# A seven-product matrix multiply and its seam: weight differences and splits from GpSimd to VectorE, and a product reordered by token tile

## The chip, the cores and the metric

The kernel runs on one core of a Trainium2 chip. A core has a matrix engine (TensorE, PE in the profile, with its weight loads as PEld), a vector engine (VectorE, DVE), a scalar engine (ScalarE, ACT), a general engine (GpSimd, POOL) and a queue that issues transfers between the chip's main memory and the on-chip memory (SyncE, SP). Each engine works through its own instructions in a fixed order and waits on semaphores for the others. Matrix results land in PSUM, in banks of 128 x 512 float32; all else lives in SBUF. The metric is the time on the device in microseconds (us), the median over runs.

## The reference

One layer of a bidirectional encoder over 1024 tokens of width 1024, in float32. Each of its three sub-layers is wrapped in RMS norms, and the normed result is added to the residual:

```
x = x + rms(mix(rms(x)) @ w_out)                  # window attention and gated DeltaNet, in parallel
c = softmax(q k^T / 16) v @ w_co                  # 4-head cross-attention to 256 memory tokens
x = x + rms(c) * g_cross_post
f = (silu(h @ w_gate) * (h @ w_up)) @ w_down      # h = rms(x) * g_ffn_pre
x = x + rms(f) * g_ffn_post
```

The change touches the product with `w_co` (1024 x 1024), the norm and residual behind it, and what prepares its result for the feed-forward part.

## The kernel before

**Splits.** Every float32 matrix product is made of three products of rounded parts. `split(hi, lo, src)` (lines 100 to 107) lets ScalarE cast the source to the rounded part `hi` (L103) and another engine subtract it from the source to get `lo` (L104): VectorE, unless the caller names GpSimd with `eng=`. `three` (L1254) then adds hi x hi, hi x lo and lo x hi into one bank. So each operand costs one ScalarE and one VectorE or GpSimd instruction before TensorE can use it.

**The w_co product.** Tokens, inner dimension and output columns are each halved, and the four blocks of the activations (q0, q1, of the two token halves) and of the weights (b11, b12, b21, b22) are combined by a scheme that needs seven block products instead of eight, with sums and differences of blocks around them. A block product is 512 tokens (four token tiles of 128) x 512 inner rows (four of 128, `HK`) x 512 columns: 48 matmuls into four banks. In order they are: a11 with B11 and a12 with B21 (both with weights loaded as they are), s3 with b12, a22 with b21, the s2 part with b22, s1 with b11, and s4 with B22 loaded again. Between the first ones, `sums` and `later` form the weight differences in place, four steps of two each; each is one `minus` of 128 x 512 (L1275), sixteen in all, on GpSimd. `weight_part` (line 1237) splits one 128 x 512 row block of a formed weight; its parts come from a ring of nine slots, tag `wpart`, and it is marked as more urgent than its place in the program. `act_part` splits the activation blocks in the same way, two row blocks at a time.

**The order of the loops.** `block_product` goes over the four inner row blocks outside and the four token tiles inside, so all four banks are complete only in the last quarter. The last product (s4) is written out by hand with the token tiles outside: each bank is complete before the next one begins.

**Finishing a token tile.** When the last term of a tile is in, VectorE adds it up (L1318), ScalarE squares it for the norm (`square_of`, L1279), the post gain is multiplied in (L1321), and `finish` loads the residual (L1288, SP), forms the reciprocal root of the mean square on GpSimd in two tiny steps (L1290 and L1291), adds the scaled tile to the residual on VectorE (L1292), stores it (L1293, SP), squares the sum on ScalarE (L1295), forms the second reciprocal root on GpSimd (L161 and L162) and scales, on ScalarE for even tiles (L1299) and VectorE for odd ones (L1301). The second half of the tokens (tiles 4 to 7, in `zl`) is finished behind the s1 product, the first half (`zz`) behind s4.

**The seam.** The code behind it turns these tiles with TensorE transposes (L1376), eight groups of the tokens in `zl` first, each group needing all four tiles. For `zl`, ScalarE multiplies in the gain (L1387) and each group is split into x1h and x1l, the `lo` part on GpSimd for even groups and VectorE for odd ones. For `zz`, four steps form X22 and the sums T1 to T4 that the seven-product scheme of the feed-forward part needs; the `lo` parts of T2 and T4 are made on GpSimd. Beside this, the first four column blocks of the feed-forward product that need only x1h and x1l (`EARLY`, banks `pA`, L1421) already run.

**What sets the order.** The instructions of one engine run in the order a planner writes at compile time, from a model of their times and the urgency of each; it is not changed at run time. Weight loads (`load_w`, L126) and weight and activation parts are marked as urgent by 300 places.

Of the kernel before, what the change touches and what calls it, by code (L numbers as in the profile page):

```python
# [14 lines left out]
ALU = mybir.AluOpType  # L15
# [4 lines left out]
P = 128  # L20
# [56 lines left out]
def tile_hybrid_block(  # L77
# [22 lines left out]
    def split(hi, lo, src, scale=None, eng=None):  # L100

        if scale is None:
            nc.scalar.copy(hi, src)  # L103
            (eng or nc.vector).tensor_tensor(lo, src, f32(hi), ALU.subtract)  # L104
        else:
            nc.scalar.activation(hi, src, AF.Identity, scale=scale)
            nc.vector.scalar_tensor_tensor(lo, src, scale, f32(hi), ALU.mult, ALU.subtract)
# [1129 lines left out]
    def weight_part(b_, k):  # L1237
        with tc.high_priority(AHEAD):
            dh, dl = (rg.tile([P, HALF], F32R, tag="wpart", name="wpart", bufs=9) for _ in range(2))
            split(dh, dl, b_[:, k])  # L1240
        return dh, dl
# [14 lines left out]
    def block_product(banks, a, b_, first=True, last=True, extra=None):  # L1256

        for k in range(HK):
            if k % 2 == 0:
                ah, al = act_part(a, k)  # L1260
            if isinstance(b_, tuple):
                if k % 2 == 0:
                    rows, c0 = (HK * b_[0] + k) * P, HALF * b_[1]
                    wh, wl = load_w(w_co[rows:rows + 2 * P, c0:c0 + HALF], 2, HALF)
                dh, dl = wh[:, k % 2], wl[:, k % 2]
            else:
                dh, dl = weight_part(b_, k)
            for t in range(4):
                three(banks[t], ah[:, k % 2], al[:, k % 2], dh, dl, slice(t * P, (t + 1) * P), first and k == 0,
                      last and k == HK - 1, first and last)  # L1270
            if extra:
                extra(k)

    def minus(o_, a, b_):
        nc.gpsimd.tensor_tensor(o_, a, b_, ALU.subtract)  # L1275

    def square_of(src, ch, r):
        jk = tz.tile([P, HALF], F32, tag="junk", name="junk")
# [2 lines left out]
    def finish(r, z, eng):  # L1281

        tok = slice(r * P, (r + 1) * P)
        if 4 <= r < 6:
            xr = xr45[:, r - 4]
        else:
            xr = tz.tile([P, D], F32, tag="xr", name="xr", bufs=2)
        nc.sync.dma_start(xr, d_x1[tok, :])  # L1288
        rs = tz.tile([P, 1], F32, tag="prs", name="prs", bufs=4)
        nc.gpsimd.tensor_scalar(rs, ssq[:, 1, r:r + 1], ssq[:, 0, r:r + 1], D * EPS, ALU.add, ALU.add)  # L1290
        nc.gpsimd.tensor_tensor(rs, rs, mhalf[:, 0:1], ALU.pow)  # L1291
        nc.vector.scalar_tensor_tensor(xr, z, rs, xr, ALU.mult, ALU.add)  # L1292
        nc.sync.dma_start(d_x2[tok, :], xr)  # L1293
        s2 = tz.tile([P, 1], F32, tag="ps2", name="ps2", bufs=4)
        nc.scalar.activation(z, xr, AF.Square, accum_out=s2)  # L1295
        r2 = tz.tile([P, 1], F32, tag="pr2", name="pr2", bufs=4)
        rstd_of(r2, s2, 1.0 / D, EPS)
        if eng is nc.scalar:
            nc.scalar.activation(z, xr, AF.Identity, scale=r2)  # L1299
        else:  # L1300
            nc.vector.tensor_scalar(z, xr, r2, None, ALU.mult)  # L1301
# [15 lines left out]
    def add(o_, a, b_):  # L1317
        nc.vector.tensor_tensor(o_, a, b_, ALU.add)  # L1318
# [31 lines left out]
        add(e_[:, t], e_[:, t], X[t])  # L1350
    xr45 = opB3.tile([P, 2, D], F32, tag="b30", name="xr45")
    Z = four([PG] * 4)
    block_product(Z, s1_, b11, last=False)
    for t in range(4):
        add(za[:, t], za[:, t], Z[t])
        square_of(za[:, t], 1, 4 + t)
        gained(za[:, t], za[:, t], HI, nc.vector)
        finish(4 + t, zl[:, t], (nc.scalar, nc.vector)[t % 2])
# [26 lines left out]
    for k in range(KT):  # L1385
        pt = turned_k(first_rows, k)
        nc.scalar.activation(raw[:, k, :], pt, AF.Identity, scale=gain("ffn", k))  # L1387
        split(x1h[:, k, :], x1l[:, k, :], raw[:, k, :], eng=(nc.gpsimd, nc.vector)[k % 2])
    tr = LR2.enter_context(pool("tr", 1, side="right"))
    T2, T4 = (blocks(t) for t in operand(opA, "s0"))  # L1390
    T1, T3 = (blocks(t) for t in operand(opB, "s2"))
# [2 lines left out]
    for k in range(HK):  # L1394
        p0, p1 = turned_k(last_rows, k), turned_k(last_rows, k + HK)
        g0, g1 = gain("ffn", k), gain("ffn", k + HK)
        x12, t1, t2_, t3_ = (tr.tile([P, HALF], F32, name=f"r{i}", tag=f"r{i}") for i in range(4))
        t4 = raw[:, k + HK]
        nc.scalar.activation(x12, p0, AF.Identity, scale=g0)
        nc.vector.scalar_tensor_tensor(t1, p0, g0, raw[:, k], ALU.mult, ALU.subtract)  # L1400
        nc.vector.scalar_tensor_tensor(t3_, p1, g1, x12, ALU.mult, ALU.subtract)
        nc.vector.scalar_tensor_tensor(t2_, p1, g1, t1, ALU.mult, ALU.subtract)
        split(X22[0][:, k], X22[1][:, k], p1, g1)
        split(T1[0][:, k], T1[1][:, k], t1)
        split(T3[0][:, k], T3[1][:, k], t3_)
        nc.vector.tensor_tensor(t4, t4, t2_, ALU.subtract)
        split(T2[0][:, k], T2[1][:, k], t2_, eng=nc.gpsimd)
        split(T4[0][:, k], T4[1][:, k], t4, eng=nc.gpsimd)


    NF = FF // P
# [343 lines left out]
```

## Time and profile before

| | |
|---|---|
| median of three runs | 1540.01 us (1538.43 to 1542.44) |
| profiled execution | 1542.75 us, span 1541.0 us |
| mean granted TensorE clock | 0.987 |
| busy: TensorE, VectorE, ScalarE, GpSimd | 1479.5, 1106.6, 746.9, 436.5 us |
| w_co product (L1254) in the span | 766 to 873.5 us |
| seam and early feed-forward blocks | 873.5 to about 944 us |

A row of a group of instructions names line, engine, operation and tiles (out<-in), then shape and count, busy time and mean ns of one, and the idle time of that engine just before them with what ended it. A row of the timeline begins with the start and the length in us. A row of the waits says who waited for whom: total us, times, longest. A row of busy time by stretch gives the stretch, its length, the busy time and the number of instructions of each engine, the granted clock (1.00 is full), the DMA share and GB/s. A row of one tile gives shortest, median and longest ns, and the first and last start.

### The profile page before, as it was taken

The page shows a single profiled execution, that of the slowest core. Times are in us where ns is not written, and L with a number is a line of the kernel's source. Part 1 is how long each engine was busy: PE and PEld are TensorE (multiplying, and loading weights), DVE is VectorE, ACT ScalarE, POOL GpSimd, SP SyncE. Part 2 cuts the span into 40 slices and gives each one's busy share as a digit, 9 for nine tenths or more (in the row PEclk, how much of TensorE's full clock was granted, in tenths as well). Part 3 has the DMA queues.
Part 4 walks back from the last instruction along what each step waited for, and adds up shares of the span by engine and source line. Part 5 has one row for each costly group of instructions (what it writes and reads, how often), then busy time and mean ns, then how long its engine had stood idle before and what let it go on. Part 6 is the DMA issues. An engine that isn't in the chain of part 4 may idle for free.

```text
span 1541.0 us, 21093 instructions
## 1 busy us (share of the span) xinstructions
PE 1479.5 (96%) x7403; PEld 1242.7 (81%) x7403; DVE 1106.6 (72%) x1766; ACT 746.9 (48%) x1524; POOL 436.5 (28%) x432
## 2 busy tenths in 40 slices
PE   6999999998999899999989798999999999999998
PEld 5888888877989778888878677888888888888786
DVE  6868999786889865535388766776867554696665
ACT  5578821457567663555445574323223332454532
POOL 2020221311336103342160734343433332000021
PEclk9999999999999999999999899999999999999999
DMA  6235575857996674431332354333533333853355
GB/s 206 76 105 150 145 192 157 215 158 189 323 301 209 218 253 164 162 112 58 109 108 69 127 200 131 123 126 113 166 125 100 109 103 103 314 209 99 109 176 166
DMA packets 264167, 241.91 MB, mean 157 GB/s; under 512 B 33768, under 2 KB 203645, under 8 KB 264061
## 3 DMA queue, kind: packets, MB, share of 16 engines
q1 hardware_dynamic: 264061, 240.57, 49.9%
q8 instruction: 58, 0.95, 0.3%
q14 instruction: 48, 0.39, 0.1%
HBM read 171.02 MB, written 66.88 MB: 154 GB/s over the span
## 4 chain that ended last, share of the span: by engine, by line
PE 69%; DVE 10%; DMA 8%; ACT 5%; issue 3%; POOL 2%; SPq 2%; DVEq 0%; POOLq 0%; ACTq 0%
PE pD L1421 8%; PE pE L1421 8%; PE pA L1421 7%; PE pcq L261 6%; PE pmg L1068 6%; PE pdX L1612 6%; PE pg L261 5%; PE pB L1421 4%; PE pst L1254 4%; PE psc L809 3%; PE pdA L1612 2%; PE pdX L1709 2%; PE pdD L1612 2%; DVE acc L286 2%; PE pco L1183 1%
## 5 line engine op out<-in xcount | busy, mean ns | idle before, releaser
L103 ACT CAST whi<-wraw 128x1024 fp32r<-128x1024 f32 x98 | 102.8, 1050 | 154.2 <-issue 39.9
L104 POOL TENSOR_TENSOR wlo<-wraw,whi 128x1024 fp32r<-128x1024 f32 x38 | 91.5, 2409 | 185.2 <-ACT whi L103 185.2
L261 PE MATMUL pg<-hlo,whi 128*128 128x512 f32 x352 | 139.8, 397 | 0.0
L261 PE MATMUL pg<-hhi,whi 128*128 128x512 f32 x352 | 139.2, 396 | 0.0
L261 PE MATMUL pg<-hhi,wlo 128*128 128x512 f32 x352 | 138.6, 394 | 0.0
L1421 PE MATMUL pA<-b,whi 128*128 128x512 f32 x352 | 112.7, 400 | 3.4 <-POOL b L104 1.8
L104 DVE TENSOR_TENSOR wlo<-wraw,whi 128x1024 fp32r<-128x1024 f32 x60 | 77.1, 1287 | 41.9 <-ACT whi L103 39.4
L1421 PEld LDWEIGHTS pA<-b,whi 128*128 128x128 f32 x352 | 66.2, 191 | 18.9 <-POOL b L104 2.5
L1612 PE MATMUL pdX<-dhl,whi 128*128 128x512 f32 x264 | 76.1, 390 | 1.5 <-DVE zv L1671 0.7
L261 PEld LDWEIGHTS pg<-hhi,whi 128*128 128x128 f32 x352 | 66.6, 190 | 13.5 <-ACT hhi L103 0.2
L261 PEld LDWEIGHTS pg<-hlo,whi 128*128 128x128 f32 x352 | 66.5, 189 | 12.8
L261 PEld LDWEIGHTS pg<-hhi,wlo 128*128 128x128 f32 x352 | 66.5, 189 | 12.9
L1499 POOL TENSOR_TENSOR act<-act,up 128x512 f32<-128x512 f32 x33 | 49.9, 1511 | 93.7 <-DVE up L1498 62.2
L1421 PE MATMUL pA<-b,wlo 128*128 128x512 f32 x176 | 69.4, 396 | 0.5 <-DVE wlo L104 0.5
L103 ACT CAST whi<-araw 128x1024 fp32r<-128x1024 f32 (+1 forms) x36 | 35.3, 981 | 68.4 <-PE pdX L1612 24.4
L1646 POOL TENSOR_SCALAR frs<-sq 128x1 f32<-128x1 f32 x8 | 12.0, 1498 | 194.3 <-ACT jk L1631 193.4
L104 DVE TENSOR_TENSOR wlo<-araw,whi 128x1024 fp32r<-128x1024 f32 (+1 forms) x36 | 40.8, 1134 | 35.1 <-ACT whi L103 34.9
L286 DVE SCALAR_TENSOR_TENSOR acc<-cp,cols,acc 128x1024 f32<-128x1024 f32 x48 | 62.1, 1296 | 0.1
L1612 PEld LDWEIGHTS pdX<-dhl,whi 128*128 128x128 f32 x264 | 49.3, 188 | 12.7 <-issue 1.1
L1421 PE MATMUL pB<-s,s1h 128*128 128x512 f32 x176 | 54.5, 390 | 3.1 <-ACT s1h L103 3.1
L1472 DVE TENSOR_TENSOR sr<-sr,wraw 128x512 f32<-128x512 f32 x22 | 36.7, 1667 | 27.8 <-POOL sr L1471 27.8
L1471 POOL TENSOR_TENSOR sr<-wraw 128x512 f32<-128x512 f32 x22 | 29.9, 1358 | 91.9 <-DMA wraw<-in_w_gate_up_dram 91.9
(471 smaller groups left out, 4329.2 us busy)
## 6 DMA issues: line engine op xcount, KB each, us to landing
wraw<-in_w_gate_up_dram SPq DMA_DIRECT2D x52, 512.0 KB, 3.9
kv<-d_kv SPq DMA_DIRECT2D x32, 512.0 KB, 7.0
wraw<-in_w_in_dram SPq DMA_DIRECT2D x22, 512.0 KB, 5.0
b<-in_w_down_dram SPq DMA_DIRECT2D x20, 512.0 KB, 7.9
araw<-d_as SPq DMA_DIRECT2D x20, 512.0 KB, 3.7
pz<-d_pz SPq DMA_DIRECT2D x32, 256.0 KB, 6.8
wraw<-in_w_ckv_dram SPq DMA_DIRECT2D x16, 512.0 KB, 5.1
wraw<-in_w_out_dram SPq DMA_DIRECT2D x16, 512.0 KB, 3.7
```

The source lines that it names most:

```text
L103: nc.scalar.copy(hi, src)
L104: (eng or nc.vector).tensor_tensor(lo, src, f32(hi), ALU.subtract)
L261: nc.tensor.matmul(p_, w[:, k, :], ah[a][:, k, :], start=(k == 0 and i == 0), stop=(k == nk - 1 and i == 2))
L286: nc.vector.scalar_tensor_tensor(acc, cp[:, t:t + S], taps[t], acc, ALU.mult, ALU.add)
L809: nc.tensor.matmul(out[:, d, h, :], lt[:, d, h, :], rt[:, d, h, :], start=True, stop=True)
L1068: nc.tensor.matmul(pp[t], act[a][:, k, tt], w_[:, kk, :], start=(k == 0 and i == 0), stop=(k == KT - 1 and i == 2))
L1254: nc.tensor.matmul(bank, a[:, tt], w, start=(start and i == 0), stop=(stop and i == 2), skip_group_check=not check)
L1421: nc.tensor.matmul(out_, w[a][:, k, :], xx[b_][:, k, :], start=(start and k == 0 and i == 0), stop=(k == HK - 1 and i == 2), skip_group_ch ...
L1472: nc.vector.tensor_tensor(s[1], s[0], a_[:, 0:HK], ALU.subtract)
L1499: nc.gpsimd.tensor_tensor(o_, o_, up, ALU.mult)
L1612: nc.tensor.matmul(banks[t], a[:, k - k0, tt], w, start=(first and k == 0 and i == 0), stop=(k == NB - 1 and i == 2), skip_group_check=not ...
L1709: nc.tensor.matmul(X[t], a[:, k], w[:, k0 + k], start=False, stop=(k0 + k == NB - 1 and i == 2), skip_group_check=True)
```

## The change

The sixteen weight differences (`minus`) go from GpSimd to VectorE. So does the first of the two tiny steps in `finish` (L1290), eight times. The product of s1 with b11 (behind those with b12, b21 and b22) is no longer made by `block_product`: both activation parts and all four weight parts are asked for first, and then the four token tiles are the outer loop, each going through the four inner row blocks and being added up, squared and finished before the next one begins in the program. In the seam, the `lo` parts of all eight groups of x1 and of T2 and T4 are made on VectorE: four and eight instructions of 128 x 512 that were on GpSimd. Sums, products, transfers and buffers are the same.

```
     def minus(o_, a, b_):
-        nc.gpsimd.tensor_tensor(o_, a, b_, ALU.subtract)
+        nc.vector.tensor_tensor(o_, a, b_, ALU.subtract)
...
-        nc.gpsimd.tensor_scalar(rs, ssq[:, 1, r:r + 1], ssq[:, 0, r:r + 1], D * EPS, ALU.add, ALU.add)
+        nc.vector.tensor_scalar(rs, ssq[:, 1, r:r + 1], ssq[:, 0, r:r + 1], D * EPS, ALU.add, ALU.add)
         nc.gpsimd.tensor_tensor(rs, rs, mhalf[:, 0:1], ALU.pow)
...
     Z = four([PG] * 4)
-    block_product(Z, s1_, b11, last=False)
+    acts = [act_part(s1_, k) for k in (0, 2)]
+    wts = [weight_part(b11, k) for k in range(HK)]
     for t in range(4):
+        for k in range(HK):
+            three(Z[t], *(h[:, k % 2] for h in acts[k // 2]), *wts[k], slice(t * P, (t + 1) * P), k == 0, False, False)
         add(za[:, t], za[:, t], Z[t])
         square_of(za[:, t], 1, 4 + t)
...
-        split(x1h[:, k, :], x1l[:, k, :], raw[:, k, :], eng=(nc.gpsimd, nc.vector)[k % 2])
+        split(x1h[:, k, :], x1l[:, k, :], raw[:, k, :], eng=nc.vector)
...
-        split(T2[0][:, k], T2[1][:, k], t2_, eng=nc.gpsimd)
-        split(T4[0][:, k], T4[1][:, k], t4, eng=nc.gpsimd)
+        split(T2[0][:, k], T2[1][:, k], t2_)
+        split(T4[0][:, k], T4[1][:, k], t4)
```

## The prediction

> **What bounds the kernel now.** I read the page first. All numbers are in us from the start of the profiled execution, which took 1542.75 (span 1541.0); the median of the three runs is 1540.01, so the profiled one is 2.7 slow, and I take differences off its span and apply them to the median.
>
> ```profile
> span 1541.0 us, 21093 instructions
> PE 1479.5 (96%) x7403; PEld 1242.7 (81%) x7403; DVE 1106.6 (72%) x1766; ACT 746.9 (48%) x1524; POOL 436.5 (28%) x432
> ```
>
> TensorE is busy for 96%. Only 61 us of idle time and whatever it runs at a lower clock are to be had. The next view is the busy time by stretch around w_co and the seam; columns after the stretch: its length, then busy time (instructions) of PE, weight loads, VectorE, ScalarE, GpSimd, then the granted clock, DMA share, GB/s.
>
> ```profile
> 766.00:785.00 19.00, 19.00 (x106) 16.40 (x105) 11.90 (x19) 6.49 (x18) 10.57 (x8) 1.00 0.69 238
> 785.00:796.00 11.00, 6.33 (x28) 5.69 (x28) 10.93 (x12) 5.50 (x13) 11.00 (x8) 0.69 0.12 44
> 796.00:850.00 54.00, 54.00 (x258) 45.02 (x257) 48.07 (x76) 32.07 (x63) 8.70 (x6) 1.00 0.19 59
> 850.00:873.50 23.50, 23.49 (x104) 19.13 (x102) 19.42 (x28) 8.78 (x21) 17.55 (x18) 1.00 0.31 123
> 873.50:891.00 17.50, 9.02 (x28) 6.55 (x29) 10.62 (x13) 15.63 (x29) 14.58 (x19) 0.61 0.58 197
> 891.00:902.20 11.20, 11.12 (x59) 8.52 (x58) 6.28 (x7) 8.71 (x16) 5.31 (x6) 1.00 0.66 235
> 902.20:958.00 55.80, 50.61 (x229) 39.97 (x228) 42.17 (x56) 32.99 (x53) 18.23 (x13) 1.00 0.49 152
> 958.00:1290.00 332.00, 332.00 (x1467) 274.89 (x1466) 231.70 (x280) 100.66 (x162) 133.83 (x84) 1.00 0.37 118
> ```
>
> TensorE has two holes: 785 to 796 (4.7 idle) and 873.5 to 891 (8.5 idle), both at a reduced mean clock; 902 to 958 is a porous stretch with 5.2 idle. From 958 TensorE is full for 332 us, so time won before it moves everything after it. The waits of TensorE name the holes, and the clock by single microseconds shows their tail.
>
> ```profile
> PE ptn L1376 <- ACT zl L1299: 5.8, 2, 5.3
> PE pct L1173 <- DVE cs L1193: 3.9, 1, 3.9
> PE pA L1421 <- POOL b L104: 1.8, 1, 1.8
> ```
>
> ```profile
> 788.00:789.00 1.00, 0.00 (x0) 0.00 (x0) 0.97 (x3) 0.00 (x0) 1.00 (x1) 0.77 0.00 0
> 795.00:796.00 1.00, 1.00 (x5) 0.79 (x5) 0.96 (x3) 0.00 (x0) 1.00 (x2) 0.82 0.00 0
> 890.00:891.00 1.00, 1.00 (x4) 0.80 (x3) 0.58 (x1) 0.39 (x1) 0.71 (x2) 0.53 0.57 229
> ```
>
> The clock falls to one half inside each hole and stays there for some 5 us after work is back in the first (to 795), some 10 in the second (to 891).
>
> **Edit 1: sixteen weight differences from GpSimd to VectorE.** They now fill GpSimd, and VectorE beside them is stretched. The rows: the differences, the weight splits that read them and the matmuls that read those; VectorE between 780.05 and 790.3, ending at the L1193 that TensorE waits for; and the same forms undisturbed.
>
> ```profile
> L1275 POOL TENSOR_TENSOR wco<-wco x16: 1267/1709/2274, 774.4 to 797.7; 128x512 f32<-128x512 f32 x16
> L104 DVE TENSOR_TENSOR wpart<-wco,wpart x16: 682/685/1767, 778.9 to 855.8; 128x512 fp32r<-128x512 f32 x16
> L1254 PE MATMUL pst<-wpart,b x144: 387/389/481, 815.2 to 862.2; 128*128 128x512 f32 x144
> ```
>
> ```profile
> L1167 DVE TENSOR_TENSOR cpr<-cpr,csum 128x512 f32<-128x512 f32 x2 | 3.3, 1654 | 0.0
> L1160 DVE TENSOR_SCALAR cmx<-cmx 128x2 f32<-128x2 f32 x2 | 2.5, 1252 | 0.0
> ...
> L104 DVE TENSOR_TENSOR wpart<-wco,wpart 128x512 fp32r<-128x512 f32 x1 | 1.8, 1759 | 0.0
> ...
> L1193 DVE TENSOR_TENSOR cs<-oraw,pco 128x512 f32<-128x512 f32 x1 | 0.7, 675 | 0.0
> ```
>
> ```profile
> L1167 DVE TENSOR_TENSOR cpr<-cpr,csum 128x512 f32<-128x512 f32 x4 | 2.8, 688 | 0.1
> ```
>
> ```profile
> L1160 DVE TENSOR_SCALAR cmx<-cmx x16: 149/170/2075, 691.0 to 806.6; 128x2 f32<-128x2 f32 x16
> ```
>
> A difference costs VectorE 0.685 (the L104 form on the same tile), 16 x 0.685 = 11.0 in all. What it gives back ahead of L1193: two L1167 at 1.654 instead of 0.688 (1.93), two L1160 at 1.252 instead of 0.170 (2.16), one weight split at 1.759 instead of 0.685 (1.07): 5.2. L1193, with one operand in PSUM, is not stretched. The differences' first reader on TensorE starts at 815.2, but weight splits ask for them ahead; I put four ahead of L1193 (2.7), net 2.5 earlier. The idle 4.7 shrinks to 2.2. The clock fell in the 789th microsecond, about 2 after TensorE stopped (790.45 - 3.89 = 786.56 in the row below); with the gap nearly as short as those 2 I count the low clock as gone (4.8 us at half speed lost 2.4). So 2.5 + 2.4 = 4.9, less 0.4 for a fuller VectorE in 796 to 850 (48.07 of 54 busy): **4.5 won**. The ends: 4.7 + 2.4 = 7.1 won if the hole closes; 11.0 - 5.2 = 5.8 lost if all sixteen stand ahead of L1193 and nothing after it gains. I sit near the first end since TensorE does not need the results for 25 us after the hole.
>
> ```profile
> 790.45 1.12 PE L1173 MATMUL pct<-ident,cpr 128*128 128x128 f32 x4 [3.89 <-DVE cs L1193]
> ```
>
> The Trainium skill, "SBUF — State Buffer", section "Who interferes with whom", says that a VectorE instruction with two SBUF inputs, or in a two-port mode, is shut out while a GpSimd instruction that reads SBUF holds the shared port pair. The trace agrees: L1167 and the split go to 1.654 and 1.759, L1193 stays at 0.675. By that rule alone the stretch ahead of L1193 goes entirely and the sum for this edit is between the 2.5 above and 5.2 before the clock; the rest of the argument uses the rows.
>
> **Edit 2: the s1 product, one token tile after another.** Rows of the order in time, in the seam:
>
> ```profile
> 851.57 11.04 PE L1254 MATMUL pst<-wpart,b 128*128 128x512 f32 x48
> 855.80 0.68 DVE L104 TENSOR_TENSOR wpart<-wco,wpart 128x512 fp32r<-128x512 f32 x1
> 861.29 2.48 DVE L1318 TENSOR_TENSOR zl<-zl,pst 128x512 f32<-128x512 f32 x4 [3.01 <-PE pst L1254]
> 872.82 1.15 ACT L1299 ACTIVATE zl<-xr,pr 128x1024 f32<-128x1024 f32 x1 [3.07 <-POOL pr L162]
> 879.06 1.15 ACT L1299 ACTIVATE zl<-xr,pr 128x1024 f32<-128x1024 f32 x1
> 880.26 1.11 PE L1376 MATMUL ptn<-ident,zl 128*128 128x128 f32 x4 [5.27 <-ACT zl L1299]
> ```
>
> Now the four banks complete together at 861 to 862.6, so four finish chains (add, square, two GpSimd steps, scaled add with the residual, square, two GpSimd steps, scaling) start together and the third one's scaling ends at 880.2; TensorE left its last product at 873.5. With the tile loop outside, a bank completes each 11.04 / 4 = 2.76: about 854.3, 857.1, 859.8, 862.6. The first chain took 861.29 to 873.97 = 12.7 with all four queued on GpSimd; so the last takes at most that.
>
> The price: tile 0 now needs all four weight pairs at once. Nine slots serve the pairs of two products, and the eighth part needs a slot that the product before frees at its end, 851.57. Its split ran at 855.80, behind nine adds of the evictions. Tile 0 wants it after 10 of its 12 matmuls, at 851.57 + 10 x 0.23 = 853.9; if VectorE's order stays, TensorE stands until 856.5: 2.6 lost (0 if the split is put first; 4.5 if it goes behind all twelve adds, three more at 0.6). I take 2.6. The last bank is then complete at 865.2 and its scaling at 877.9 at worst, against an end of the next product at 873.5 + 2.6 = 876.1: the long wait before the transposes goes.
>
> What is late next is ScalarE. It is busy 15.63 + 8.71 = 24.3 of the 28.7 between 873.5 and 902.2. Two squares and two scalings move ahead of that:
>
> ```profile
> L1295 ACT ACTIVATE zl<-xr x4: 1040/1051/1064, 866.8 to 875.5; 128x1024 f32<-128x1024 f32 x4
> ```
>
> 2 x 1.05 + 2 x 1.15 = 4.4 less, 19.9 left. TensorE's own work there is 9.02 + 11.12 = 20.1, of which some 7.6 (880.3 to 891) ran at half clock: 16.3 at full. So the stretch cannot shrink by more than 28.7 - 19.9 = 8.8 by ScalarE, and I leave 1.8 for ScalarE's own waits. **Won with edit 3: 7.0, less 1.0** for that part of the 2.6 which ScalarE's longer queue does not cover: 6.0. Ends: 28.7 - 16.3 = 12.4 won; 2.6 lost if the chains end no earlier. The residual loads and stores of the four tiles (L1288, L1293 on SP) move ahead with them; the DMA share is 0.31 in 850 to 873.5, so I cost them nothing; if that cover fails, the reloads for tiles 0 to 3, which reuse these slots, come late.
>
> The Trainium skill, "TensorE: Matmul & The Clock Gate", Part 1, has the clock halve after about 3.4 us of idle and come back after as much sustained work. Here it halved about 2 us after the stop at 786.56 and stayed low 10 us in the second hole, so the rows are harsher than the page. By the page the gap of 2.2 that edit 1 leaves keeps the clock, and the sum below stays; by the rows it may fall, and the sum is 2.4 smaller.
>
> **Edit 3: L1290 and the four remaining even splits of x1h on VectorE.**
>
> ```profile
> L1290 POOL TENSOR_SCALAR prs<-ssq x8: 298/1048/1625, 862.9 to 884.0; 128x1 f32<-128x1 f32 x8
> ```
>
> ```profile
> L104 DVE TENSOR_TENSOR b<-oraw,b x4: 684/692/1782, 884.1 to 900.9; 128x512 fp32r<-128x512 f32 x4
> L104 POOL TENSOR_TENSOR b<-oraw,b x4: 1272/1624/2067, 885.5 to 898.1; 128x512 fp32r<-128x512 f32 x4
> L104 POOL TENSOR_TENSOR s<-r,s x4: 1306/1406/1736, 910.8 to 936.0; 128x512 fp32r<-128x512 f32 x4
> L104 POOL TENSOR_TENSOR s<-oraw,s x4: 1275/1302/1742, 912.2 to 937.2; 128x512 fp32r<-128x512 f32 x4
> ```
>
> L1290 leaves a GpSimd chain (8 x 1.05) and costs VectorE about 0.17 each, the row of L1160; the wait it adds is for ScalarE's square, with the next scaled add behind it. Four splits go from 1.62 to 0.69. Both lie in the stretch counted above (TensorE's 1.8 wait for a GpSimd split is in it), so they get no extra gain.
>
> **Edit 4: the eight splits of T2 and T4.** VectorE gets 8 x 0.69 = 5.5 in 902 to 958, where it is busy 42.17 of 55.8, GpSimd loses 8 x 1.35. TensorE waits for neither there. Cover: VectorE's 13.6 free. Ends: 5.5 lost if the cover is gone, 1.5 won if VectorE's stretched operations return to length (two or three at 1 us each). I take **1.0 lost**.
>
> Sum: 4.5 + 6.0 - 1.0 = 9.5 won. 1541.0 - 9.5 = 1531.5 of span, 1540.0 - 9.5 = **1530.5**.
>
> **Rivals.** (a) One of the two holes stays, because the written order puts the differences ahead of the softmax steps (edit 1 then 0), or because ScalarE fills the seam whatever VectorE does (edit 2 then 1.5). For it: ScalarE's 24.3 of 28.7. Against: its 4.4 do move. Gain 5 - 1 = about 4.5, 1535.5. (b) The other side: VectorE becomes the bound of 775 to 958. It gets 11.0 + 8 x 0.17 + 12 x 0.69 = 20.6 and sheds 5.2; if none of it finds a gap, 15.4 lands on its chain, less the 5.3 wait that edit 2 removes and less the 4.7 hole: +5.4, 1545.4. It decides once more than about 10 of the 20.6 stand ahead of something TensorE needs. For it: VectorE has only 5.9 idle in 796 to 850. Against: 4.1 in 850 to 873.5, 11.8 in 873.5 to 902.2 and 13.6 after. (c) The change does not do what it says: the last weight split holds the first tile (4.5 lost) and the chains still pile up on the remaining GpSimd steps; edits 2 and 3 give nothing: 4.5 - 2.6 - 1 = 0.9 won, 1539.
>
> **How the numbers follow.** A measurement of this kernel tells about 0.3% (4.6) from no change. Forecast 0.50, 1523 to 1535 by itself; (a) 0.20, half above and half below the 0.3%; (b) 0.20; (c) 0.10, a third of it slower through the 4.5 stall. Faster 0.50 + 0.10 + 0.03 of (c), where its stall is small, = 0.63; slower 0.20 + 0.03 = 0.23; same 0.10 + 0.04 = 0.14. The range reaches from both holes closed (7.1 + 12.4 - 1 = 18.5, hardly all of it: 1523) to the middle of (b), 1544.
>
> **What would show it.** Edit 1: no L1275 on GpSimd, sixteen on VectorE near 0.685, L1160 near 0.17, the wait for L1193 under 2.5 and a clock above 0.69 in that stretch. Edit 2: evictions of the s1 product's banks about 2.8 apart, a TensorE wait for a weight split of about 2.6 in its first tile, no 5.3 wait for L1299, ScalarE over 90% busy in the next 20 us. Edit 4: VectorE over 47 busy in the porous stretch with TensorE's idle near 6. Wrong if TensorE shows new waits for VectorE between 775 and 850, or if its full stretch begins later than about 950.

## The result and the profile after

The changed kernel takes 1531.33 us, median of nine runs (1530.07 to 1536.27); the kernel before, beside it, 1539.41, median of nine (1536.25 to 1543.15). The ratio is 0.9955, with a 95% interval from 0.9939 to 0.9971: 4.5 to 9.4 us faster, 6.9 by its middle (0.45%), 8.1 by the medians. Forecast were 9.5 us and 1530.5. The total came out near the forecast and a little under it; where it came from was not as forecast.

The page of the changed kernel opens with these lines:

```profile
span 1528.2 us, 21073 instructions
PE 1474.8 (97%) x7403; PEld 1236.7 (81%) x7403; DVE 1110.1 (73%) x1802; ACT 745.4 (49%) x1524; POOL 384.5 (25%) x396
```

GpSimd lost 36 instructions and 52 us, VectorE gained 36 and only 3.5 us: what moved is cheap on VectorE, and what it did already got shorter. The two profiled spans differ by 12.8, more than the runs do. The rows of two groups of matmuls, before and then after, say why (the last two numbers ahead of the shapes are the first and the last start).

```profile
L1254 PE MATMUL pst<-whi,b x96: 387/389/628, 766.2 to 873.1; 128*128 128x512 f32 x96
L1421 PE MATMUL pE<-s,bhi x176: 389/389/389, 964.4 to 1320.3; 128*128 128x512 f32 x176
```

```profile
L1254 PE MATMUL pst<-whi,b x96: 387/389/397, 760.1 to 861.4; 128*128 128x512 f32 x96
L1424 PE MATMUL pE<-s,bhi x176: 389/389/390, 950.3 to 1306.4; 128*128 128x512 f32 x176
```

The first w_co matmul starts 6.1 earlier (766.2, 760.1), ahead of anything that the change touches, and the profile of the changed kernel taken again below starts it at 767.6: that is scatter between executions. So I measure each kernel from its own marks: **w_co** from the first to the last start of the first row, the **seam** from there to the first start of the second row, behind which TensorE is full. Before: 106.9 + 91.3 = 198.2. After: 101.3 + 88.9 = 190.2. Both parts gained, 5.6 and 2.4, together 8.0, as the medians say (8.1).

Busy time by stretch, after (columns as in the prediction): the place of the first hole, the 20 us behind the end of w_co, and the whole seam. Below it are the same 20 us and the seam of the kernel before.

```profile
779.00:790.00 11.00, 10.52 (x58) 8.88 (x57) 11.00 (x20) 4.02 (x11) 0.00 (x0) 1.00 0.37 114
861.40:881.40 20.00, 14.26 (x66) 11.00 (x65) 15.45 (x23) 19.45 (x37) 6.39 (x13) 0.83 0.69 239
861.40:950.30 88.90, 78.31 (x342) 61.82 (x341) 68.13 (x94) 58.36 (x98) 20.24 (x24) 0.92 0.51 167
```

```profile
873.10:893.10 20.00, 11.51 (x43) 8.37 (x42) 11.59 (x15) 17.39 (x32) 14.92 (x19) 0.66 0.62 209
873.10:964.40 91.30, 77.54 (x342) 60.33 (x341) 62.98 (x80) 59.97 (x100) 42.36 (x40) 0.93 0.50 164
```

The first hole is gone: TensorE stands 0.5 of 11 there and keeps its full clock, with GpSimd empty. In the seam the hole is smaller, not gone: 66 matmuls and transposes in 20 us instead of 43, at a clock of 0.83 instead of 0.66. Over the whole seam TensorE is idle 10.6 instead of 13.8, but the mean clock is no higher (0.92 and 0.93): in this profile two short stretches of low clock further on, which the kernel before does not have, take back what the smaller hole saved (last section). The waits of TensorE (total, times, longest) name what is left, between 760 and 960:

```profile
PE ptn L1379 <- ACT zl L1299: 4.1, 1, 4.1
PE pA L1424 <- ACT m L1441: 2.7, 2, 2.1
PE pB L1424 <- ACT s1h L103: 2.0, 1, 2.0
```

The wait for L1193 has left the list. The wait for L1299, which the prediction had going, is still its first entry, 4.1 instead of 5.3.

### The profile page after: what moved, and what is told of

It is laid out like the page before. It is cut to its first block, busy times and chain, and to the rows that moved or that the text cites. A ratio compares the mean times of both kernels' runs of the same rounds, so it can differ in the third digit from the quotient of the medians.

```text
span 1528.2 us, 21073 instructions
## 1 busy us (share of the span) xinstructions
PE 1474.8 (97%) x7403; PEld 1236.7 (81%) x7403; DVE 1110.1 (73%) x1802; ACT 745.4 (49%) x1524; POOL 384.5 (25%) x396
## 4 chain that ended last, share of the span: by engine, by line
PE 67%; DVE 11%; DMA 10%; ACT 6%; issue 3%; SPq 2%; POOL 1%; DVEq 0%; POOLq 0%; ACTq 0%
PE pD L1424 8%; PE pE L1424 8%; PE pA L1424 7%; PE pcq L261 6%; PE pmg L1068 6%; PE pdX L1615 6%; PE pg L261 4%; PE pB L1424 4%; PE pst L1254 4%; PE pdA L1615 2%; PE psc L809 2%; PE pdD L1615 2%; DVE acc L286 2%; DMA qr<-d_q 1%; DVE wlo L104 1%
## 5 line engine op out<-in xcount | busy, mean ns | idle before, releaser
L1424 PEld LDWEIGHTS pA<-b,whi 128*128 128x128 f32 x352 | 66.4, 191 | 16.7 <-ACT m L1441 3.3
```

The lines of the kernel that those rows point to most:

```text
L1424: nc.tensor.matmul(out_, w[a][:, k, :], xx[b_][:, k, :], start=(start and k == 0 and i == 0), stop=(k == HK - 1 and i == 2), skip_group_ch ...
```

## The experiments

Each run states its median beside the kernel before on the same chip, the ratio with its interval, and the marks of its profile. The marks first, in us; the times follow run by run.

| kernel | w_co | seam | sum |
|---|---|---|---|
| before | 106.9 | 91.3 | 198.2 |
| changed | 101.3 | 88.9 | 190.2 |
| changed, once more | 101.3 | 87.9 | 189.2 |
| edit 1 alone | 100.9 | 92.7 | 193.6 |
| edit 2 alone | 106.1 | 91.6 | 197.7 |
| edit 3 alone | 105.2 | 87.7 | 192.9 |
| changed, without edit 2 | 101.1 | 88.2 | 189.3 |
| changed, L1290 back on GpSimd | 103.4 | 92.3 | 195.7 |
| changed, x1h splits back | 101.1 | 91.9 | 193.0 |
| changed, without edit 4 | 102.7 | 87.3 | 190.0 |
| changed, with extra GpSimd reads | 106.6 | 88.7 | 195.3 |
| changed, without edits 2 and 4, casts reordered | 102.5 | 87.3 | 189.8 |
| changed, differences behind head 0's splits | 99.6 | 88.6 | 188.2 |
| the last, without edits 2 and 4 | 99.6 | 87.5 | 187.1 |

The two rows of the changed kernel show how far two profiles of the same program part: 0 in w_co, 1.0 in the seam. A difference under 1 in the seam is not read as an effect. Where the differences stay on GpSimd and nothing in the first hole is edited, w_co is 106.9, 106.1 and 105.2, so 1.7 there is scatter too; the differences on VectorE are below all three.

**Edit 1 alone.** The kernel before with the sixteen differences on VectorE:

```
     def minus(o_, a, b_):
-        nc.gpsimd.tensor_tensor(o_, a, b_, ALU.subtract)
+        nc.vector.tensor_tensor(o_, a, b_, ALU.subtract)
```

> The kernel before with edit 1 alone (the sixteen weight differences on VectorE). Theory: edit 1 closes the first hole by itself. TensorE's wait for L1193 falls from 3.9 us to under 1, the clock stays at 1.00 through the differences, VectorE's L1160 and L1167 are back at 0.17 and 0.69 us, and w_co (first matmul of its first product to the last of its last) is 5 to 6 us shorter than the 107.0 us of before; the wait of over 5 us for L1299 in the seam stays; time 1533 to 1535. Rival: the gain belongs to the tile order, edit 1 gives less than 2.5 us and the time is above 1536.5.

Measured: 1535.42 against 1541.07, ratio 0.9963 (0.9948 to 0.9978). It takes 6.0 off w_co, the whole of what the changed kernel gains there; the seam is no better than before. The time lies 0.4 above the theory's band. TensorE's longest wait for L1299 is 3.4 instead of over 5, with another of 2.3 for L1301 in the same hole.

**The changed kernel without edit 2.** `block_product` for s1 again:

```
-    acts = [act_part(s1_, k) for k in (0, 2)]
-    wts = [weight_part(b11, k) for k in range(HK)]
+    block_product(Z, s1_, b11, last=False)
     for t in range(4):
-        for k in range(HK):
-            three(Z[t], *(h[:, k % 2] for h in acts[k // 2]), *wts[k], slice(t * P, (t + 1) * P), k == 0, False, False)
```

> The changed kernel with the s1 product back in its old loop order. Theory: VectorE is behind by then (its adds for the product before run until 848.6, when three of the four banks of the s1 product are complete), so the order of the tiles gives nothing: time within 1.5 us of the changed kernel (1530 to 1533), the four evictions start within 0.5 us of where they do in the changed kernel. Rival, as predicted: the tile order is worth about 6 us, and the time goes to 1536 or more.

Measured: 1534.69 against 1541.07, ratio 0.9954 (0.9935 to 0.9972), the ratio of the changed kernel. The median lies 1.7 above the theory's band, in runs that spread from 1529.8 to 1539.1; the marks sum to 189.3, between the two profiles of the changed kernel. So no loss without the new order is seen. VectorE of the changed kernel shows why: four tiles' evictions of the s1 product (start, length, group):

```profile
840.26 1.28 DVE L104 TENSOR_TENSOR wpart<-wco,wpart 128x512 fp32r<-128x512 f32 x2
841.46 0.67 DVE L1318 TENSOR_TENSOR zl<-zl,pst 128x512 f32<-128x512 f32 x1
...
848.04 0.67 DVE L1318 TENSOR_TENSOR p<-p,pst 128x512 f32<-128x512 f32 x1
848.64 1.87 DVE L1318 TENSOR_TENSOR zl<-zl,pst 128x512 f32<-128x512 f32 x3
850.92 0.69 DVE L1318 TENSOR_TENSOR zl<-zl,pst 128x512 f32<-128x512 f32 x1 [0.41 <-PE pst L1254]
```

and without edit 2:

```profile
849.57 0.68 DVE L1318 TENSOR_TENSOR p<-p,pst 128x512 f32<-128x512 f32 x1
850.42 2.73 DVE L1318 TENSOR_TENSOR zl<-zl,pst 128x512 f32<-128x512 f32 x4 [0.16 <-PE pst L1254]
```

The banks do complete one after another, but between the last weight splits (840.26) and 848.64 VectorE works off the twelve additions of the product before, without a pause. The first three banks wait for it and are added back to back; only the fourth comes after its bank. Against the end of w_co (861.4 and 862.9) the additions of this product begin 12.8 ahead with edit 2 and 12.5 without: 0.3 earlier, and no more.

**Edit 2 alone.** The kernel before with the token-tile order and nothing else.

> The kernel before with the tile order of the s1 product alone. As predicted: a TensorE wait of about 2.6 us for the last weight split in the first tile, then no long wait for L1299, net 3 to 6 us faster than before. Theory now: VectorE's adds hold the evictions until 6.6 us after the first bank is complete, so the chains start hardly earlier; no wait for the weight split above 1 us, the wait for L1299 stays above 3.5 us, and the stretch from the start of w_co to pE is within 2 us of the 198.2 of before.

Measured: 1542.74 against 1540.66, ratio 1.0016 (1.0004 to 1.0028), slightly slower if anything; w_co 106.1, seam 91.6. With GpSimd still in the chains it gives nothing either.

**Does GpSimd's reading make the first hole?** The changed kernel with 64 subtractions of 128 x 128 on GpSimd, four behind each difference, into a tile that nobody reads. TensorE's instructions in w_co are the same, and up to the hole and past it (37 us) they come in the same order.

```
+    def beside(b_):
+        for c in range(4):
+            nc.gpsimd.tensor_tensor(dmy, b_[:, c * P:(c + 1) * P], ident, ALU.subtract)
     def sums(k):
         minus(b11[:, k], b12[:, k], b11[:, k])
+        beside(b11[:, k])
...
```

> The changed kernel with 64 extra GpSimd subtractions of 128 x 128 beside the differences (each reads the difference just made and a constant, and writes a scratch tile that nobody reads; nothing waits for them). Theory of the shared port: VectorE's operations with two SBUF operands in that stretch grow again (L104 and L1167 over 0.9 us mean, some over 1.2), the first hole opens again in part and the time rises by 2 to 7 us over the changed kernel. Rival: before, it was only the slow GpSimd that handed the differences late to the weight splits; then nothing changes, VectorE's operations stay at 0.68 us and the time within 1.5 us.

Measured: 1539.36 against 1541.07, ratio 0.9986 (0.9973 to 0.9999); w_co 106.6. First the changed kernel, VectorE between 767 and 784, then the same with the extra reads, with TensorE's wait as the last line.

```profile
767.36 4.91 DVE L1275 TENSOR_TENSOR wco<-wco 128x512 f32<-128x512 f32 x8 [3.08 <-DMA wco<-in_w_co_dram]
774.60 0.68 DVE L104 TENSOR_TENSOR cpl<-pct,cph 128x512 fp32r<-128x512 f32 x1
...
781.81 0.67 DVE L1193 TENSOR_TENSOR cs<-oraw,pco 128x512 f32<-128x512 f32 x1
...
783.07 1.21 DVE L104 TENSOR_TENSOR wlo<-wraw,whi 128x1024 fp32r<-128x1024 f32 x1
```

```profile
769.23 6.52 DVE L1275 TENSOR_TENSOR wco<-wco 128x512 f32<-128x512 f32 x8 [3.41 <-DMA wco<-in_w_co_dram]
779.12 0.68 DVE L104 TENSOR_TENSOR cpl<-pct,cph 128x512 fp32r<-128x512 f32 x1
...
783.86 1.48 DVE L104 TENSOR_TENSOR wlo<-wraw,whi 128x1024 fp32r<-128x1024 f32 x1
...
788.20 0.68 DVE L1193 TENSOR_TENSOR cs<-oraw,pco 128x512 f32<-128x512 f32 x1
```

```profile
779.85 0.78 PE L1183 MATMUL pco<-cph,vr 128*128 128x512 f32 x1 [3.42 <-DVE cpl L104]
```

Eight differences take 6.52 instead of 4.91, the weight split 1.48 instead of 1.21; cpl and L1193, which have an operand in PSUM, keep their 0.68. What queues behind the stretched ones comes late, and TensorE waits 3.42 for cpl instead of 0.43, and its clock falls: 5.3 of the 5.6 that edit 1 had won in w_co are lost again, with VectorE's own work unchanged. Only 0.3 of it can be the load of the weights, which VectorE waits for in the first line of each view. So stretched VectorE instructions alone are enough for a hole of this size. It is not the old hole itself, which was a wait for L1193 under another written order of TensorE's instructions; the changed order with the differences still on GpSimd was not run. The Trainium skill, "SBUF — State Buffer", section "Who interferes with whom", has the rule (two SBUF inputs against a GpSimd instruction that reads SBUF), and this pair of runs agrees with both halves of it.

**L1290 back on GpSimd.** The changed kernel with that line as before.

> The changed kernel with L1290 back on GpSimd. Theory (the splits hold the gain): the seam stretch stays within 1 us of 88.9 and the time within 1.5 of the changed kernel. Rival (L1290 holds it): the stretch is 91 to 94 and the wait for L1299 is over 6 us.

Measured: 1538.02 against 1540.66, ratio 0.9981 (0.9968 to 0.9995); the seam 92.3, as the rival had it. Its sign, a wait for L1299 of over 6, did not come: the hole is split between L1301 and L1299. A part of the time is not the seam's: w_co is 103.4, a late load (below). Transposes of TensorE behind w_co (start, length, group, idle before), with L1290 on GpSimd and then as changed:

```profile
873.21 0.69 PE L1379 MATMUL ptn<-ident,zl 128*128 128x128 f32 x2 [2.30 <-DVE zl L1301]
877.13 1.11 PE L1379 MATMUL ptn<-ident,zl 128*128 128x128 f32 x4 [3.23 <-ACT zl L1299]
```

```profile
862.61 0.44 PE L1379 MATMUL ptn<-ident,zl 128*128 128x128 f32 x2 [0.62 <-DVE zl L1301]
867.15 1.12 PE L1379 MATMUL ptn<-ident,zl 128*128 128x128 f32 x4 [4.11 <-ACT zl L1299]
```

The last of these groups starts 877.13 - 869.6 = 7.5 behind the end of w_co instead of 867.15 - 861.4 = 5.7. The longer hole also costs clock: 0.74 in the 20 us behind w_co instead of 0.83. On GpSimd the step took 0.62 at the median and 2.28 at most here, on VectorE 0.21 every time:

```profile
L1290 POOL TENSOR_SCALAR prs<-ssq x8: 294/622/2277, 859.7 to 879.6; 128x1 f32<-128x1 f32 x8
```

```profile
L1290 DVE TENSOR_SCALAR prs<-ssq x8: 204/206/209, 852.1 to 869.8; 128x1 f32<-128x1 f32 x8
```

**The x1h splits back.** The changed kernel with the four even splits on GpSimd.

> The changed kernel with the even splits of x1h back on GpSimd. The stretch from the last matmul of w_co to the first matmul that reads bhi (pE) was 91.3 us before, 88.9 in the changed kernel and 92.7 with edit 1 alone, so edit 3 must hold about 4 to 6 us of the seam. Theory: the four x1h splits on GpSimd are most of it, since TensorE's early blocks read them; this run has a stretch of 91 to 94 and a time of 1533.5 to 1536. Rival: it is L1290, which took GpSimd time ahead of every finish chain; then the stretch stays below 90 and the time at 1530 to 1533.

Measured: 1537.05 against 1540.66, ratio 0.9977 (0.9966 to 0.9989); the seam 91.9, in the theory's band, and the time 1 above its band. The hole behind w_co is the same as in the changed kernel (4.10). The loss comes later: the last of the eight splits starts 24.6 behind the end of w_co (890.0 - 865.4) instead of 22.0 (883.4 - 861.4).

```profile
L104 POOL TENSOR_TENSOR b<-oraw,b x4: 1270/1284/1290, 874.5 to 885.9; 128x512 fp32r<-128x512 f32 x4
L104 DVE TENSOR_TENSOR b<-oraw,b x4: 679/692/693, 878.1 to 890.0; 128x512 fp32r<-128x512 f32 x4
```

```profile
L104 DVE TENSOR_TENSOR b<-oraw,b x8: 681/684/693, 870.3 to 883.4; 128x512 fp32r<-128x512 f32 x8
```

The first two lines are with the splits back on GpSimd, the third is the changed kernel. How these 3.0 come about is not shown: no single wait of TensorE in this profile is longer by as much.

**Edit 3 alone.** The kernel before with these two lines:

```
-        nc.gpsimd.tensor_scalar(rs, ssq[:, 1, r:r + 1], ssq[:, 0, r:r + 1], D * EPS, ALU.add, ALU.add)
+        nc.vector.tensor_scalar(rs, ssq[:, 1, r:r + 1], ssq[:, 0, r:r + 1], D * EPS, ALU.add, ALU.add)
...
-        split(x1h[:, k, :], x1l[:, k, :], raw[:, k, :], eng=(nc.gpsimd, nc.vector)[k % 2])
+        split(x1h[:, k, :], x1l[:, k, :], raw[:, k, :], eng=nc.vector)
```

> The kernel before with edit 3 alone: L1290 and the four even splits of x1h on VectorE; the weight differences and the T2/T4 splits stay on GpSimd, the s1 product stays block by block. Theory (edit 3 carries the gain in the seam, alone): w_co as before, 106 to 107, the seam 85.5 to 88 (91.3 before), first w_co matmul to first pE matmul 192.5 to 195 (198.2), ratio 0.9965 to 0.998. Rival (the two steps pay only once the tile order and the differences have made room for them): the seam 90 to 91.5, 196.5 to 198.5, ratio 0.999 to 1.0.

Measured: 1537.52 against 1542.63, ratio 0.9977 (0.9961 to 0.9993); the seam 87.7, w_co 105.2, the sum 192.9. The theory's numbers for the seam, the sum and the ratio hold; w_co came out 0.8 under them. What it has less of in w_co lies at the first hole, which edit 3 does not touch (0.8 less idle time, and half as long a stretch of low clock), so the 3.6 of the seam is what edit 3 gives. In the 20 us behind w_co this kernel looks like the changed one, with the differences still on GpSimd and the old order of s1 in it:

```profile
877.10:897.10 20.00, 14.03 (x66) 10.64 (x66) 14.21 (x23) 18.86 (x36) 8.45 (x12) 0.83 0.66 229
```

**Without edit 4.** The changed kernel with the splits of T2 and T4 on GpSimd.

> The changed kernel with the splits of T2 and T4 back on GpSimd. Theory: these eight splits fill VectorE in the porous stretch and cost about 2 us there: time 1528.5 to 1530.5, and the stretch from the second early block to the first pB matmul is 1.5 to 2.5 us shorter than in the changed kernel. Rival: GpSimd's reads stretch VectorE's operations as before, and it is the same or up to 1 us slower.

Measured: 1531.74 against 1541.07, ratio 0.9934 (0.9919 to 0.9948). The time is 1.2 above the theory's band. The seam is 87.3, 0.6 and 1.6 under the two profiles of the changed kernel; from the end of w_co to the first pB matmul it is 66.4, against 67.1 and 68.1. Edit 4 costs about 1, hardly outside the scatter. The 1.6 contains a stretch of low clock more (13.7 in the seam against 10.2 here); with the same low clock it is 0.6, and 1.1 between the last two kernels of the table (6.8 each), which differ by edit 2 as well. Its w_co is 102.7, which belongs to the load of the next study.

**The wait for L1299.** The third tile's scaling stands behind other work on ScalarE, though the GpSimd step that it needs ends at 862.87 + 0.55 = 863.4. Changed kernel, that step and then ScalarE:

```profile
862.87 0.55 POOL L162 TENSOR_TENSOR pr<-pr,mhalf 128x1 f32<-128x1 f32 x1
```

```profile
862.41 1.03 ACT L103 CAST whi<-wraw 128x1024 fp32r<-128x1024 f32 x1
863.35 1.05 ACT L1295 ACTIVATE zl<-xr 128x1024 f32<-128x1024 f32 x1
864.31 0.19 ACT L1295 ACTIVATION_READ_ACCUMULATOR zl<-xr 128x1 f32 x1
864.40 1.03 ACT L103 CAST whi<-wraw 128x1024 fp32r<-128x1024 f32 x1
865.34 0.63 ACT L1279 ACTIVATE junk<-zz 128x512 f32<-128x512 f32 x1
...
865.96 1.14 ACT L1299 ACTIVATE zl<-xr,pr 128x1024 f32<-128x1024 f32 x1
```

ScalarE has no gap here. From 863.4 on stand ahead of L1299 the fourth tile's square, a weight cast for the feed-forward part (another was made just before) and a square of the other token half; 2.5 of the 4.1 that TensorE waits pass that way. The kernel before had much of this already. There the third tile's GpSimd step ends at 876.48 + 0.55 = 877.0, and two such casts and a square still stand ahead of its L1299 at 879.06, so 2.0 of that wait of 5.3 was ScalarE's queue:

```profile
876.48 0.55 POOL L162 TENSOR_TENSOR pr<-pr,mhalf 128x1 f32<-128x1 f32 x1
```

```profile
876.57 1.03 ACT L103 CAST whi<-wraw 128x1024 fp32r<-128x1024 f32 x1
...
878.13 1.03 ACT L103 CAST whi<-wraw 128x1024 fp32r<-128x1024 f32 x1
```

In the next kernel, without edits 2 and 4, the two weight loads of the first column block are ordered behind the third tile's scaling (`scaled`, which `finish` now returns):

```
...
-            whi, wlo = load_w(w_gate_up[:, c0:c0 + P], KT, P)
+            with tc.issue_after(scaled.ins) if e == 0 else ExitStack():
+                whi, wlo = load_w(w_gate_up[:, c0:c0 + P], KT, P)
```

> The changed kernel with the s1 product in its old order, the T2 and T4 splits on GpSimd, and the two ScalarE casts of the first gate_up weights made to stand behind the third tile's scaling L1299, which TensorE's transposes wait for. Theory: that wait is 4.1 us in the changed kernel because these casts (2 x 1.0 us) stand ahead on ScalarE though the scaling's input is there at 863.4; it falls to about 2 us. With the 1.6 to 2 us of the T2 and T4 splits the stretch from the start of w_co to pE is 185.5 to 188 instead of 190.2 and the time 1526 to 1529.5. Rival: the early blocks then wait as long for those casts, and only the 2 us of T2 and T4 are won (188 to 189).

Measured: 1532.1 against 1540.66, ratio 0.9950 (0.9932 to 0.9968). The wait fell to 2.5, but neither the sum (189.8) nor the time reached the theory's band; w_co is 102.5, a late load (next study). The seam stayed at the 87.3 of the kernel without edit 4: TensorE now waits 1.5 for L1387 (0.4 without the reordering) and 1.3 for splits of b (nothing). The wait moved to what the reordering put behind.

**The wait that edit 1 adds.** VectorE stands at the first difference until the w_co weights have landed, with head 0's two splits of cpl queued behind it. In the kernels with w_co from 100.9 to 101.3 that wait was 2.6 to 3.1; in those from 102.5 to 103.4 it was 4.3 to 4.5, as here (the changed kernel without edit 4, VectorE and then TensorE):

```profile
777.81 4.91 DVE L1275 TENSOR_TENSOR wco<-wco 128x512 f32<-128x512 f32 x8 [4.54 <-DMA wco<-in_w_co_dram]
...
785.04 0.68 DVE L104 TENSOR_TENSOR cpl<-pct,cph 128x512 fp32r<-128x512 f32 x1
```

```profile
785.78 0.50 PE L1183 MATMUL pco<-cph,vr 128*128 128x512 f32 x1 [1.90 <-DVE cpl L104]
```

To test it, all sixteen differences of the changed kernel are ordered behind head 0's second split of cpl in the second token half (`last_pl` lists these splits in program order):

```
...
     def minus(o_, a, b_):
-        nc.vector.tensor_tensor(o_, a, b_, ALU.subtract)
+        with tc.issue_after(last_pl[9].ins):
+            nc.vector.tensor_tensor(o_, a, b_, ALU.subtract)
```

> The changed kernel with one edit: the sixteen weight differences ordered behind head 0's second split of cpl in the second token half. Theory (VectorE stands at the first difference for the wco load, with head 0's splits behind it, and passes a part of that wait on to TensorE): no wait of VectorE for the wco load at a difference ahead of those splits, TensorE's wait for cpl is 0, w_co 100 to 101.3, the seam as in the changed kernel (88.9), ratio 0.994 to 0.996. Rival (that wait is covered in the fast case, and the differences now come later than the weight splits want them): w_co 102.5 or more, a new TensorE wait for a weight split.

Measured: 1535.08 against 1542.17, ratio 0.9945 (0.9925 to 0.9966). The splits now come first and the differences wait for nothing:

```profile
776.49 0.69 DVE L104 TENSOR_TENSOR cpl<-pct,cph 128x512 fp32r<-128x512 f32 x1 [4.55 <-ACT cph L103]
777.70 0.68 DVE L104 TENSOR_TENSOR cpl<-pct,cph 128x512 fp32r<-128x512 f32 x1
778.29 2.48 DVE L1277 TENSOR_TENSOR wco<-wco 128x512 f32<-128x512 f32 x4
```

TensorE no longer waits for cpl, and w_co is 99.6, 1.7 under the changed kernel and 0.4 under the theory's band. TensorE has no idle time left in w_co, against 0.9 in the changed kernel (0.4 for cpl, 0.5 for a weight split). Its written order is a different one here too, and the other 0.8 is not accounted for. The times do not resolve so little. The changed kernel with nothing edited ran beside it:

> The changed kernel once more, with nothing edited, for the scatter between profiles. Theory (the length of w_co follows the landing of the wco load): w_co either 101.3 or less with VectorE's wait for the load at 3.1 or less, or 102.5 to 103.4 with 4.3 or more; the seam 88 to 89.5 in both cases; ratio 0.9945 to 0.997. Rival (w_co's two lengths belong to the edits of the kernels that showed them): w_co 101.3 again whatever that wait.

Measured: 1533.57 against 1542.17, ratio 0.9946 (0.9931 to 0.9961). Its wait for the load was 3.1 and w_co 101.3, the same as in its first profile: it landed in the early case again, which both theories allow. That a late landing lengthens the unedited kernel was not seen; that the wait for cpl goes when VectorE's order is changed was, in the run before.

**A better version.** The same order of the differences, without edits 2 and 4.

> The changed kernel with three edits: the s1 product again block by block (four token tiles per weight pair), the T2/T4 splits again on GpSimd, and the sixteen weight differences, still on VectorE, ordered behind head 0's second split of cpl in the second token half, so that the wait for the wco load has nothing of TensorE's next products behind it. Theory (edit 1 and edit 3 carry the gain, edit 4 costs about 1.6, the tile order about 0.7, the wait for the wco load 0 to 2): w_co takes 100 to 101.3 however late the load lands, the seam 87 to 87.5, first w_co matmul to first pE matmul 187 to 188.8 (190.2 in the changed kernel); time 1527 to 1530.5, ratio about 0.992 to 0.994, below the changed kernel. Rival (the differences now delay the weight splits of the first products, or the one is given back in the seam as with the reordered casts): 190 or more, ratio 0.995.

Measured: 1531.48 against 1542.17, ratio 0.9929 (0.9911 to 0.9948). Its marks sum to 187.1, 2.1 to 3.1 under the two profiles of the changed kernel and as the theory had it; w_co is 0.4 under its band, and the time 1.0 above. The median lies 2.1 below the changed kernel on the same chip, and the intervals overlap: faster than before for certain, faster than the change by the marks, which the times alone do not settle. Its seam also happens to hold less low clock (6.8) than the changed kernel's two (13.7 and 10.2).

## Why the prediction was right, and where it was wrong

**The total.** Forecast 9.5 won; 8.1 by the first set of medians, 8.6 by the second (1542.17 - 1533.57), 8.0 to 9.0 by the marks. The interval of the ratio (4.5 to 9.4) ends just under the forecast. By place, 4.5 was forecast for w_co and 6.0 - 1.0 = 5.0 for the seam; 5.6 and 2.4 to 3.4 were measured (the 5.6 is 3.9 against the shortest w_co with the differences on GpSimd). So the second was sized high, the first by these profiles low, and the errors in part cancel: that the total is so near is in part luck. And the seam's term, "won with edit 3" but worked out from the tile order alone, belongs to edit 3.

**Edit 1: right, sized a little low.** 4.5 forecast; 5.6 in w_co inside the change, 6.0 there and 4.6 over both parts by itself. The wait for L1193 went and the clock stayed at 1.00, as in the forecast's better end: TensorE's idle time in w_co is 0.9 instead of 4.7, where 2.2 were to be left. The run with extra reads shows that a stretched VectorE alone costs about as much. The step "I put four ahead of L1193" is wrong: fourteen of the sixteen stand ahead of it. By the prediction's own sum that was nearly its losing end (5.8 lost). It did not happen, as far as the traces tell, for two reasons. VectorE had idle time there for a good part of them: the prediction's row of 766 to 785 has it busy for 11.90 of 19, and the sum looked at 780 to 790 alone. And TensorE's written order moved, with 18 instead of 11 w_co matmuls ahead of head 0's work and the transposes that waited for L1193 some 6 us later. No run separates the two from the stretch. What was left out is the wait for the w_co load at the first difference, with the cpl splits behind it: 0.4 of TensorE's time in the changed profile and 1.9 in another.

**Edit 2: the failed step.** "6.0 won" was 0 within the scatter: removing it leaves the ratio at 0.9954, doing it alone gives 1.0016. Three of its parts fell. The sequence of banks "854.3, 857.1, 859.8, 862.6" was taken as the sequence of the chains, but a chain begins with VectorE's addition, and VectorE is full with the twelve additions of the product before; rival (b)'s row, 5.9 idle in 796 to 850, had said so. The stall of 2.6 for the eighth weight split did not come: the planner put that split (840.26) ahead of those additions, and they are what fills VectorE until 848.64. And "the long wait before the transposes goes" did not: 4.1 of 5.3 stayed. The part of it that stands behind ScalarE's queue was 2.0 before and is 2.5 now; the prediction put the whole wait down to the chains, and named ScalarE as late next without applying it to L1299 itself.

**Edit 3: "no extra gain" was the seam's gain.** Alone it takes 3.6 off the seam (5.3 off the sum of the marks and 5.1 off the median, with 1.7 of scatter at the first hole). Taking one of its halves back costs the changed kernel 3.4 to 4.4 (L1290) or 3.0 to 4.0 (the splits). Taking both back, with edits 2 and 4, costs 3.8 to 4.8 in the seam (edit 1 alone, 92.7). So the halves do not add up: either one missing gives up most of it. The prediction had both facts in its rows, L1290 at 1.05 in a chain of two GpSimd steps and the splits at 1.62 with a TensorE wait of 1.8, and booked them under edit 2 because they lie "in the stretch counted above". A stretch counted once is right; which edit it hangs on was not asked.

**Edit 4.** 1.0 lost was forecast, about 1 (0.6 to 1.6) was seen. The sign "VectorE over 47 busy in the porous stretch" failed: it is 42.69 of 55.8 (896.2 to 952.0 after), in a stretch of the same length. The two stretches do not hold quite the same work, so this counts for little.

**The signs.** Those of edit 1 came true, those of edit 2 did not, but for ScalarE, over 90% busy. Of the two signs of being wrong, new waits for VectorE between 775 and 850 did appear, of 0.4 (cpl) and 0.5 (a weight split), too short to turn the result; the full stretch began at 950.3, at the line.

**The rivals.** (a), one hole stays, was nearest in mechanism: most of the long L1299 wait did stay, and ScalarE is busy 19.45 of 20 behind w_co. Its time, 1535.5, was not reached: w_co gained in full, and edit 3 shortened the seam. (Its "5 - 1 = about 4.5" does not add up: its own terms, 0 + 6.0 - 1.0 or 4.5 + 1.5 - 1.0, give 5.0.) (b), VectorE as the bound, was half true: it is full from 840 to 861 but for 0.4, and took from edit 2 what that was to win, but the kernel did not get slower. (c) was right that the chains still start together, though on VectorE's additions and not on GpSimd's steps, and its stall was wrong.

## What to carry to other kernels

A reordered product frees results earlier only if the engine that takes them out of PSUM is free at that moment: look at its row in the microseconds in question, not at the bank's completion. When several edits meet in one stretch, count the stretch once, but ask of each edit whether the gain survives without it; here the large edit gave nothing and the two small ones gave the seam. Where one engine's result comes late, look at what stands ahead of the step that reads it as well: the queue was there before the change. And a transfer's wait that is moved to another engine brings its queue with it: put the operations that TensorE needs next ahead of the one that waits.

## What was not expected of the hardware

- 64 small GpSimd reads (0.78 each at the median), beside VectorE instructions with both inputs in SBUF, cost the kernel 5.3 us in w_co without one more instruction on VectorE; instructions with one input in PSUM kept their 0.68.
- The clock in the seam, changed kernel, by single microseconds (those in which it falls and comes back, in the hole and 50 us later):

```profile
865.00:866.00 1.00, 0.00 (x0) 0.00 (x0) 0.56 (x1) 1.00 (x4) 0.41 (x1) 0.94 0.07 20
872.00:873.00 1.00, 1.00 (x5) 0.94 (x5) 1.00 (x3) 1.00 (x2) 0.00 (x0) 0.65 0.74 221
923.00:924.00 1.00, 1.00 (x5) 0.82 (x6) 0.90 (x1) 0.62 (x1) 1.00 (x2) 0.95 0.38 143
927.00:928.00 1.00, 0.43 (x2) 0.00 (x0) 0.53 (x1) 0.00 (x0) 0.00 (x0) 0.84 0.00 0
```

  In the hole it falls at about 865.9, 2.8 after TensorE stopped (862.61 + 0.44), and is back at about 872.7, 5.5 after work resumed at 867.15: 6.8 at one half. Later it falls at 923.9 and is back at 927.3, after a gap of only 2.1 (920.77 to 922.83), and when work had been back for 1.1: 3.4 at one half. So the gap of about 2 at which the prediction's rows and rule parted did occur, though not in the first hole, and here it cost clock. In the second profile of the changed kernel the gap in that place, 2.3 long (928.6 to 930.9), cost none.
- The low clock comes in pieces of one length. Added up over single microseconds, it lasts 6.8, 10.2, 13.7 or 17.1 in the seam of every one of the fourteen profiles: two, three, four or five times 3.4. The prediction's "about 2" after the stop and 5 or 10 after work is back are the ends of pieces of 6.8 and 13.7. The two profiles of the changed kernel, 1.0 apart in the seam, differ by one piece (13.7 and 10.2), which at half speed is worth about that. What sets where a piece begins is not shown here.
- Two-input VectorE operations of 128 x 512 in a row overlap: 0.68 each by their rows, 4.91 for eight, 0.60 apart.
- The start of w_co moves by 7.5 us from one profile to the next of the same program (760.1 and 767.6), with nothing changed ahead of it. Two spans should not be subtracted without a mark behind that scatter.
